# Larger step budgets in attention slots 9 to 17, smaller ones from slot 18 on, and four output-projection items behind one gate

## The chip, the cores and the metric

The kernel runs on one core of one Trainium2 chip. The metric is device time in microseconds (us); lower is better. A profile of one execution gives, for every instruction, its start and its length on one of five engines: PE (TensorE: matrix products, with the weight loads counted apart as PEld), DVE (VectorE), ACT (ScalarE), POOL (GpSimd) and SP (which issues the DMAs). Each engine works through its own instructions in program order; semaphores make one engine wait for another.

## The reference, cut to what matters

One layer of a hybrid encoder is computed for 512 prompt rows and 64 sample rows (576 in all, width 1024). Two kinds of attention stand side by side: four differential heads (two softmax maps each) and four latent heads, whose queries, keys and values are first expanded from normalised latents. Both go into one output projection, and a gated feed-forward network follows.

```
proj = h @ w_in
q_d, k_d = rope(...), rope(...); v_d = ...              # differential heads
c_q, c_kv = rmsnorm(...), rmsnorm(...); k_r = rope(...) # latents, shared rotary key
q_m = c_q @ w_qb;  kv = ckv_all @ w_kvb                 # latent heads, expanded
od = (softmax(s0) - lam * softmax(s1)) @ v              # per differential head
om = softmax(q_nope k_nope^T + q_rope k_rope^T) @ v     # per latent head
x1 = x + concat(od, om) @ w_out
y  = x1 + (silu(conv(g)) * u) @ w_down
```

## The kernel before

Everything is float32; the large products are made of three products of split operands (a high part and a rest), so each product of a 128-row weight tile is a group of three matrix instructions (lines 138 to 140). The attention part is scheduled by hand: under `manual_schedule` the order of the code is the order on each engine.

Attention is a list of 36 blocks (128 queries each, or the sample rows): first 18 differential blocks (`ND` is 18), then 18 latent ones. They pass through a pipeline of slots. In one slot the block before last finishes, the last one is transposed, and a new one begins:

- `combine` (DVE) joins or scales the probabilities of the previous block; `begin` makes the scores of the new one (PE: `S` or `Sm`), their maximum (DVE: `nmax`) and their exponential (ACT: `p`);
- `transpose` turns the previous block's probabilities (PE: `tp`, DVE copy: `pT`);
- `values` multiplies the block before that with its values (PE: `O`, `Os` or `Om`), and after a head's last block a normalisation follows (`osq` on ACT, `orn` on POOL, `ob` and `mixd` on DVE, `ot` on PE).

After each of these three, `Filler.run(us)` puts in products that do not depend on the block, so that PE has something to do while DVE and ACT work on the softmax. They come from the list `fill`, in this order: V0, K1, Q1, V1 (values, keys and queries of differential heads), CQ, CKV, KR (the query latent, the key/value latent and the shared rotary key), QU (rotary part of the latent queries), U0, U1 (expansion of latent heads 0 and 1), VM (values of the latent heads), U2, U3, W0 to W3 (the half of the output projection that the differential heads feed). Each item is cut into steps; a step carries a cost in us by the number of its columns, and `run` takes steps until its budget is used. The budgets stand in `GAPS`: six rows of three, one row for each stretch of slots.

```
gap = GAPS[(slot > ND // 4) + (slot >= ND // 2) + (slot >= 3 * ND // 4) + (slot >= ND) + (slot >= ND + 9)]
filler.need(*needs.get(slot, ()))
```

So the rows hold for slots 0 to 4, 5 to 8, 9 to 12, 13 to 17, 18 to 26 and from 27 on. `needs` says what has to be complete before a slot may begin: before slot 18, the first with latent scores, CQ, CKV, KR, QU and U0; whatever of them is left is issued there in one piece. An item named in `gates` is passed over until the gate is lifted: VM until the last differential block has given its values (slot 19), W0 until slot 20. At the start of W0 `residual()` issues the four DMAs that bring x again.

Some work rides along with the steps: the splitting of weights that later items need (`wqr`, `wqn`, `wkv`, `wo`: high part on ACT, rest on DVE or POOL), and chains called sides, that are moved on by one at every few steps (normalising and splitting the latents: `lsq`, `ncol`, `rc`, `rbc`, `lc`, `lat`; splitting the rotary key and queries: `kr`, `qr`). The products of the fill list share three PSUM buffers under the tag `acc`, and `ncol` and `rbc` of the sides use the same three; a fourth product waits until DVE or ACT has read the oldest.

Of the kernel before, what the change touches and what calls it, by code (L numbers as in the profile page):

```python
# [36 lines left out]

GAPS = ((1.0, 1.0, 1.0), (1.2, 1.2, 1.2), (0.8, 1.2, 1.2), (0.9, 0.9, 0.9), (0.8, 1.1, 1.1), (0.9, 1.0, 0.9))  # L40
NORM_STEPS = (3, 1, 4, 2)
LATE_STEPS, ROPE_STEPS, KEY_STEPS, ROW_STEPS, FIRST_WEIGHTS = 10, 2, 4, 3, 3
SPLIT_EVERY = {"V1": 3, "U1": 2, "KR": 2, "CKV": 3, "QU": 3, "U0": 2}
# [21 lines left out]
def stream_step(ctx: ExitStack, tc: tile.TileContext, i, o):  # L65
# [34 lines left out]
    class Weights:  # L100
        def __init__(self, src, n, name, parts=1, raw=None, own=None):
            self.raw = raw_tile(name + "r") if raw is None else raw
            self.ready = self.begun = False
            if own is None:
                self.place(name)
            else:
                self.hi, self.lo = own
            self.cols = parts if isinstance(parts, list) else [
                slice(n * m // parts, n * (m + 1) // parts) for m in range(parts)]
            self.src = src  # L110
            if parts == 1 and raw is None:
                self.load()
# [824 lines left out]
    class Filler:  # L937
        def __init__(self):
            self.credit = 0.0
            self.count = 0  # L940
            self.name = "start"
            self.done = set()
            self.gates = {"VM", "W0"}
            self.sides = []
            self.gen = None
            self.specs = [w for item in fill for w in item[1]]
            self.loaded, self.todo = [], []
            for _ in range(3):
                self.load()
# [99 lines left out]
    filler = Filler()  # L1049
# [40 lines left out]
    if True:  # L1090
        filler.need("V0")
        tails = []

        def resume():
            for t in list(tails):
                if next(t, "end") == "end":
                    tails.remove(t)

        at = {}
        for n, blk in enumerate(blocks):  # L1100
            at[n, 0] = blk
            at[n + 1, 1] = blk
            at[n + 2, 2] = blk
        needs = {ND // 2: ("K1", "Q1"), ND // 2 + 2: ("V1",), ND: ("CQ", "CKV", "KR", "QU", "U0"),
                 ND + 2: ("U1",), ND + 4: ("U2",), ND + 6: ("U3",)}
        for slot in range(max(k[0] for k in at) + 2):
            a, b, c = (at.get((slot, n)) for n in range(3))
            gap = GAPS[(slot > ND // 4) + (slot >= ND // 2) + (slot >= 3 * ND // 4) + (slot >= ND) + (slot >= ND + 9)]
            filler.need(*needs.get(slot, ()))
            if slot == ND:  # L1110
                filler.finish("key", "rope0")
            if slot == ND + 4:
                filler.finish("rope1")
            if b:
                b.combine()
            resume()
            if a:
                a.begin()
            filler.run(gap[0])
            if b:  # L1120
                b.transpose()
            resume()
            filler.run(gap[1])
            if c is blocks[ND]:
                filler.need("VM")
            if c:
                c.values()
            resume()
            if c and c.finish is not None:
                t = c.finish()  # L1130
                if t is not None:
                    next(t)
                    tails.append(t)
            if c is blocks[ND - 1]:
                filler.gates.discard("VM")
            if slot == ND + 2:
                filler.gates.discard("W0")
            filler.run(gap[2])
        filler.need("W3")
    order.close()  # L1140
# [458 lines left out]
```

## Time and profile before

| | |
|---|---|
| median of 3 runs | 680.38 us (680.08 to 680.64) |
| the profiled execution | 680.18 us |
| its span, first to last instruction | 678.0 us |
| busy PE / PEld / DVE / ACT / POOL | 657.3 / 632.4 / 508.4 / 314.6 / 119.5 us |
| granted PE clock, mean | 0.995 |

The span is what the profile shows from the first to the last instruction; 2.2 us of the execution lie around it. Busy times are sums of instruction lengths with overlaps removed. A matrix instruction is pipelined: its length in a row is longer than the distance to the next start, so PE that is called busy can still be fed more or less densely, but PE that is idle had nothing to do or waited. The slots do not appear in the profile by number; each begins with its score products, so slot 9 begins at 98.73 us, slot 14 at 125.93, slot 17 at 142.99, slot 18 at 166.15 and slot 22 at 190.60.

### The profile page before, as it was taken

To read this page: it belongs to the slowest core of one execution; us is meant where nothing else is said; L and a number is where in the kernel's file an instruction comes from. 1 tells how busy PE (TensorE), PEld (TensorE's weight loads), DVE (VectorE), ACT (ScalarE), POOL (GpSimd) and SP (SyncE) were. 2 spreads that over 40 slices of the span, in tenths; PEclk is the share of its full clock that TensorE was granted. 3 is DMA by queue.
4 is the path that set the end of the run, shared out by engine and by line. 5 is a ranking of instruction groups with operands and counts; after the bars stand their busy time and mean duration, and the time that the engine had idled before them with its cause. 6 is when DMAs were issued, how large, how long until landed. Compare 5 with 4: busy or idle time off the path is not lost.

```text
span 678.0 us, 12372 instructions
## 1 busy us (share of the span) xinstructions
PE 657.3 (97%) x4830; PEld 632.4 (93%) x4830; DVE 508.4 (75%) x1030; ACT 314.6 (46%) x630; POOL 119.5 (18%) x170
## 2 busy tenths in 40 slices
PE   8999999997899999999999999999999999999995
PEld 7998888996799899999999999999999999999994
DVE  5768866588667757899999859884894798697524
ACT  7424345444634345475665236432740552564152
POOL 0130213035200016152130101110110010011042
PEclk9999999999999999999999999999999999999997
DMA  8554413012514113012233303330431133114004
GB/s 286 184 164 151 133 36 113 23 32 89 201 33 155 32 32 125 1 37 89 66 123 125 125 1 124 126 112 13 143 131 38 49 109 125 54 57 143 31 1 141
DMA packets 26858, 63.63 MB, mean 94 GB/s; under 512 B 3248, under 2 KB 8304, under 8 KB 26800
## 3 DMA queue, kind: packets, MB, share of 16 engines
q1 hardware_dynamic: 26800, 62.85, 28.3%
q8 instruction: 38, 0.62, 0.4%
q14 instruction: 20, 0.16, 0.1%
HBM read 55.27 MB, written 5.21 MB: 89 GB/s over the span
## 4 chain that ended last, share of the span: by engine, by line
PE 83%; DVE 10%; ACT 3%; issue 2%; POOL 1%; DMA 1%; SPq 0%; POOLq 0%; DVEq 0%; ACTq 0%
PE yacc L138 9%; PE yacc L139 9%; PE yacc L140 9%; PE ua L1248 6%; PE ua L1246 6%; PE ua L1247 6%; PE ub L1248 3%; PE ub L1247 3%; PE ub L1246 3%; PE uc L1248 2%; PE uc L1247 2%; PE uc L1246 2%; PE uplain L138 1%; PE S L489 1%; PE uplain L139 1%
## 5 line engine op out<-in xcount | busy, mean ns | idle before, releaser
L83 DVE TENSOR_TENSOR x<-x,yacc 128x288 f32<-128x288 f32 (+2 forms) x128 | 56.3, 449 | 52.3 <-PE yacc L140 52.0
L138 PE MATMUL yacc<-act,wd 128*128 128x288 f32 x288 | 85.2, 296 | 0.0
L139 PE MATMUL yacc<-act,wd 128*128 128x288 f32 x288 | 85.1, 295 | 0.0
L140 PE MATMUL yacc<-act,wd 128*128 128x288 f32 x288 | 85.0, 295 | 0.0
L139 PEld LDWEIGHTS yacc<-act,wd 128*128 128x128 f32 x288 | 54.3, 189 | 0.0
L138 PEld LDWEIGHTS yacc<-act,wd 128*128 128x128 f32 x288 | 54.3, 189 | 0.0
L140 PEld LDWEIGHTS yacc<-act,wd 128*128 128x128 f32 x288 | 54.3, 188 | 0.0
L1274 POOL COPY cst<-G 128x2 f32<-128x2 f32 x22 | 23.1, 1052 | 166.9 <-DVE G L83 150.9
L1335 ACT COPY u<-ua 128x288 f32<-128x288 f32 x20 | 8.0, 400 | 66.9 <-PE ua L1248 66.9
L457 ACT ACTIVATE p<-S,nmax 128x128 f32<-128x128 f32 (+4 forms) x36 | 18.6, 516 | 42.1 <-DVE nmax L455 41.7
L86 DVE SCALAR_TENSOR_TENSOR conv<-G,vec,conv 128x578 f32<-128x578 f32 x44 | 35.9, 815 | 2.4 <-ACT conv L1279 2.3
L1261 POOL COPY G<-zero 128x2 f32<-128x2 f32 x22 | 9.6, 438 | 129.0 <-DVE conv L86 120.3
L83 POOL TENSOR_TENSOR n<-n,nsq 128x288 f32<-128x288 f32 x13 | 12.3, 950 | 75.1 <-ACT nsq L865 74.9
L457 ACT ACTIVATE p<-Sm,nmax 128x128 f32<-128x128 f32 (+4 forms) x18 | 9.3, 516 | 29.1 <-DVE nmax L455 29.1
L1279 ACT ACTIVATE conv<-G,vec 128x578 f32<-128x578 f32 x22 | 19.1, 870 | 7.0 <-DVE G L83 6.9
L83 POOL TENSOR_TENSOR st<-pr 128x256 f32<-128x256 f32 (+1 forms) x16 | 13.4, 858 | 49.6 <-issue 16.9
L865 ACT ACTIVATE nsq<-x 128x288 f32<-128x288 f32 (+2 forms) x28 | 12.3, 441 | 17.8 <-DVE x L83 17.7
L89 ACT CAST act<-conv 128x576 fp32r<-128x576 f32 x22 | 14.8, 675 | 11.4 <-DVE conv L83 11.3
L469 DVE COPY pT<-tp 128x128 f32<-128x128 f32 (+3 forms) x36 | 16.6, 462 | 4.3 <-PE tp L466 3.8
L1283 ACT ACTIVATE silu<-conv 128x578 f32<-128x578 f32 x22 | 15.2, 689 | 10.1 <-DVE conv L86 10.1
L455 DVE TENSOR_REDUCE nmax<-S 128x1 f32<-128x128 f32 (+4 forms) x36 | 16.9, 475 | 1.1
L466 PE MATMUL tp<-ident,p 128*128 128x128 f32 x84 | 15.3, 276 | 2.5 <-DVE p L779 1.1
(1595 smaller groups left out, 2552.7 us busy)
## 6 DMA issues: line engine op xcount, KB each, us to landing
qkT<-st SPq DMA_DIRECT2D x32, 72.0 KB, 2.1
x<-in_xT SPq DMA_DIRECT2D x4, 576.0 KB, 6.3
xraw<-in_xT SPq DMA_DIRECT2D x7, 288.0 KB, 5.9
out_kd<-st SPq DMA_DIRECT2D x4, 288.0 KB, 2.4
out_y<-x SPq DMA_DIRECT2D x3, 384.0 KB, 3.1
out_vp<-vd SPq DMA_DIRECT2D x2, 512.0 KB, 4.5
out_y<-x SPq DMA_DIRECT2D x4, 192.0 KB, 2.4
wq0r<-in_w_in SPq DMA_DIRECT2D x2, 256.0 KB, 5.7
```

Source lines behind the costliest of these rows:

```text
L83: (eng or nc.vector).tensor_tensor(out=out, in0=a, in1=b, op=op)
L86: nc.vector.scalar_tensor_tensor(out=out, in0=a, scalar=s, in1=b, op0=op0, op1=op1)
L138: nc.tensor.matmul(out, lhsT=wh, rhs=xh, start=first, stop=False)
L139: nc.tensor.matmul(out, lhsT=wh, rhs=xl, start=False, stop=False)
L140: nc.tensor.matmul(out, lhsT=wl, rhs=xh, start=False, stop=last)
L455: nc.vector.tensor_reduce(out=nmax[:, 0:1], in_=Sv, axis=AX.X, op=ALU.max, negate=True)
L457: nc.scalar.activation(out=p[:, :nk], in_=Sv, func=AF.Exp, bias=nmax[:, 0:1], accum_out=sums)
L1246: nc.tensor.matmul(acc, lhsT=wh, rhs=xh, start=first and n == 0, stop=False, skip_group_check=True)
L1247: nc.tensor.matmul(acc, lhsT=wh, rhs=xl, start=False, stop=False, skip_group_check=True)
L1248: nc.tensor.matmul(acc, lhsT=wl, rhs=xh, start=False, stop=(n == len(ks) - 1), skip_group_check=True)
L1274: nc.gpsimd.tensor_copy(out=cst[:, j, 0:2], in_=G[:, 512:514])
L1279: nc.scalar.activation(out=c[:, :578], in_=G[:, 0:578], func=AF.Identity, scale=cw[0], bias=cb)
```

## The change

The third and fourth rows of `GAPS` grow (slots 9 to 12 from 0.8, 1.2, 1.2 to 1.3, 1.5, 1.4; slots 13 to 17 from 0.9 each to 1.5, 1.5, 1.4), the fifth and sixth shrink (slots 18 to 26 from 0.8, 1.1, 1.1 to 0.8, 1.0, 1.0; from 27 on from 0.9, 1.0, 0.9 to 0.7, 0.9, 0.8). W1 to W3 now stand behind the same gate as W0, so that none of them can come before W0 and before the DMAs of x.

```diff
-GAPS = ((1.0, 1.0, 1.0), (1.2, 1.2, 1.2), (0.8, 1.2, 1.2), (0.9, 0.9, 0.9), (0.8, 1.1, 1.1), (0.9, 1.0, 0.9))
+GAPS = ((1.0, 1.0, 1.0), (1.2, 1.2, 1.2), (1.3, 1.5, 1.4), (1.5, 1.5, 1.4), (0.8, 1.0, 1.0), (0.7, 0.9, 0.8))
...
-            self.gates = {"VM", "W0"}
+            self.gates = {"VM"} | {f"W{fp}" for fp in range(4)}
...
-                filler.gates.discard("W0")
+                filler.gates -= {f"W{fp}" for fp in range(4)}
```

No instruction is added or taken away, and the order among the fill steps stays as it was but for VM: U2 and U3 are finished before its gate opens, where before it stood between them. What moves is the attention blocks among the steps. Before, when slot 18 begins, 4 steps of KR, 9 calls of QU and 5 of U0 are left and are issued in one piece. Now U0 ends in the second third of slot 17, three steps of U1 follow there, and nothing is left at slot 18.

PE, at the end of QU and the beginning of U0 (`qracc` are the rotary query products, `qnacc` the first products of U0). Before, nothing stands between them; here is the end of it and what follows:

```order
L138 MATMUL qracc<-lat,wqrh 128x320
L139 MATMUL qracc<-lat,wqrh 128x320
L140 MATMUL qracc<-lat,wqrl 128x320
L138 MATMUL qnacc<-lat,wqnh 128x256
L139 MATMUL qnacc<-lat,wqnh 128x256
L140 MATMUL qnacc<-lat,wqnl 128x256
```

Now the scores of the last differential block (slot 17, the sample rows of the second pair of heads) stand there:

```order
L138 MATMUL qracc<-lat,wqrh 128x320
L139 MATMUL qracc<-lat,wqrh 128x320
L140 MATMUL qracc<-lat,wqrl 128x320
L532 MATMUL S<-qkT 64x192 x4
L138 MATMUL qnacc<-lat,wqnh 128x256
L139 MATMUL qnacc<-lat,wqnh 128x256
L140 MATMUL qnacc<-lat,wqnl 128x256
```

In the same way the scores, transposes and value products of slots 15 and 16 have come between the products of KR and QU.

DVE, in slot 15 (`lat` is the split of the latents, `pr` the evacuation of KR's or QU's products, `wqnl` the rest of a weight split, `ob` and `mixd` the normalisation of a differential head). One piece of the difference:

```order
 L83 TENSOR_TENSOR pr<-kracc,sinr 64x256
-L83 TENSOR_TENSOR lat<-lc,lat 128x576 x2
+L505 RECIPROCAL c_1823<-sums 128x1
+L86 SCALAR_TENSOR_TENSOR c_1823<-sums,nlam,c_1823 128x1
+L86 SCALAR_TENSOR_TENSOR p<-p,c_1823 128x256
+L86 SCALAR_TENSOR_TENSOR oms<-sums 128x4
+L86 SCALAR_TENSOR_TENSOR oms<-oss,oms 128x4
+L453 MEMSET S 64x64
+L455 TENSOR_REDUCE nmax<-S 128x1
```

A block's combination and maxima now stand inside the work that KR and QU give to DVE.

DVE, further on, at the boundary of slots 15 and 16 (`c` and `p` are the combination of slot 16, `nmax` its maxima):

```order
 L83 TENSOR_TENSOR wqnl<-wqnr,wqnh 128x512 x2
 L86 SCALAR_TENSOR_TENSOR pr<-qracc,cos 128x256
 L86 SCALAR_TENSOR_TENSOR pr<-qracc,msin 128x256
+L505 RECIPROCAL c_1944<-sums 128x1
+L86 SCALAR_TENSOR_TENSOR c_1944<-sums,nlam,c_1944 128x1
+L86 SCALAR_TENSOR_TENSOR p<-p,c_1944 128x384
+L453 MEMSET S 64x64
+L455 TENSOR_REDUCE nmax<-S 128x1
+L453 MEMSET S 64x64
+L455 TENSOR_REDUCE nmax<-S 128x1
 L86 SCALAR_TENSOR_TENSOR lc<-lc,vec,rbc 128x256
 L83 TENSOR_TENSOR q<-pr 128x256
```

The instruction that writes `lc` reads `rbc` and so frees one of the three `acc` buffers; it now comes behind a whole block's combination and maxima.

## Rows read from the trace of the kernel before

**Rows 1.** The page: busy us, share and instructions; PE and clock by slice.

```profile
PE 657.3 (97%) x4830; PEld 632.4 (93%) x4830; DVE 508.4 (75%) x1030; ACT 314.6 (46%) x630; POOL 119.5 (18%) x170
...
PE   8999999997899999999999999999999999999995
...
PEclk9999999999999999999999999999999999999997
```

**Rows 2.** Stretches between slots: busy us (instructions) per engine, clock, DMA, GB/s.

```profile
98.73:142.99 44.26, 44.26 (x326) 38.63 (x325) 27.40 (x88) 20.17 (x67) 8.84 (x9) 1.00 0.17 52
142.99:166.15 23.16, 19.76 (x146) 18.01 (x145) 19.99 (x43) 12.06 (x27) 10.97 (x11) 1.00 0.26 88
166.15:190.60 24.45, 21.52 (x138) 18.17 (x138) 16.98 (x49) 15.46 (x49) 5.79 (x8) 1.00 0.39 140
190.60:224.93 34.33, 34.33 (x264) 33.74 (x263) 25.79 (x69) 12.46 (x30) 0.00 (x0) 1.00 0.30 93
```

**Rows 3.** PE's waits, 142.99 to 190.6 us: total us, times, longest.

```profile
PE qracc L138 <- DVE pr L86: 1.9, 1, 1.9
PE Sm L763 <- ACT knp L737: 1.2, 1, 1.2
PE tp L466 <- DVE p L779: 1.1, 1, 1.1
PE vmacc L747 <- ACT vm L750: 0.6, 1, 0.6
```

**Rows 4.** Timeline of PE at its longest wait: start, us, instruction, idle before.

```profile
153.59 0.38 PE L188 MATMUL rbc<-ident,rc 128*128 128x128 f32 x2
155.84 0.41 PE L138 MATMUL qracc<-lat,wqrh 128*128 128x320 f32 x1 [1.87 <-DVE pr L86]
156.09 0.31 PE L139 MATMUL qracc<-lat,wqrh 128*128 128x320 f32 x1
156.24 0.31 PE L140 MATMUL qracc<-lat,wqrl 128*128 128x320 f32 x1
```

**Rows 5.** DVE by form, 142.99 to 166.15 us: busy us, mean ns, idle before.

```profile
L83 DVE TENSOR_TENSOR lat<-lc,lat 128x576 fp32r<-128x576 f32 x3 | 3.6, 1227 | 0.0
L83 DVE TENSOR_TENSOR wqnl<-wqnr,wqnh 128x512 fp32r<-128x512 f32 x2 | 2.0, 1020 | 0.0
...
L83 DVE TENSOR_TENSOR wqrl<-wqrr,wqrh 128x512 fp32r<-128x512 f32 x2 | 1.4, 676 | 0.0
...
L86 DVE SCALAR_TENSOR_TENSOR pr<-qracc,cos 128x256 f32<-128x256 f32 x2 | 0.8, 424 | 0.0
...
L83 DVE TENSOR_TENSOR pr<-kracc,sinr 64x320 f32<-64x320 f32 x1 | 0.5, 493 | 0.0
...
L86 DVE SCALAR_TENSOR_TENSOR c<-sums,nlam,c 128x1 f32<-128x1 f32 x1 | 0.2, 220 | 0.0
...
L178 DVE TENSOR_SCALAR ms<-ncol 128x4 f32<-128x4 f32 x1 | 0.1, 143 | 0.0
```

**Rows 6.** DVE by form, 98.73 to 190.6 us: the pieces of a differential block.

```profile
L86 DVE SCALAR_TENSOR_TENSOR mixd<-ot,gsub,mixd 128x512 fp32r<-128x512 f32 x3 | 2.2, 750 | 4.4 <-ACT mixd L573 4.4
L455 DVE TENSOR_REDUCE nmax<-S 128x1 f32<-128x384 f32 x4 | 2.2, 557 | 0.1
L83 DVE TENSOR_TENSOR ob<-O,orn 128x512 f32<-128x512 f32 x3 | 2.0, 678 | 0.0
...
L469 DVE COPY pT<-tp 128x256 f32<-128x256 f32 x3 | 1.2, 413 | 0.0
...
L86 DVE SCALAR_TENSOR_TENSOR p<-p,c 128x256 f32<-128x256 f32 x2 | 1.0, 485 | 0.1
```

**Rows 7.** Timeline of POOL beside that wait.

```profile
153.42 2.62 POOL L83 TENSOR_TENSOR kro<-pr 32x320 f32<-32x320 f32 x2
```

**Rows 8.** Timeline of PE: scores, transposes, column sums, two products of QU.

```profile
130.95 0.92 PE L489 MATMUL S<-qkT 64*128 64x384 f32 x4
140.31 0.49 PE L466 MATMUL tp<-ident,p 128*128 128x128 f32 x3
149.21 1.15 PE L166 MATMUL ncol<-ones,lsq 128*128 128x1 f32 x10
...
153.23 0.28 PE L138 MATMUL qracc<-lat,wqrh 128*128 128x256 f32 x1
153.35 0.28 PE L139 MATMUL qracc<-lat,wqrh 128*128 128x256 f32 x1
```

## The prediction

> **What bounds the kernel now.** The page comes first: PE is busy for 97% of the span at full clock in all but one slice [rows 1]. Idle time of PE is therefore the only thing a reordering can win here, since the change neither adds nor removes an instruction. Next come the stretches between slots [rows 2]. PE is idle nowhere from slot 9 to slot 16 (44.26 of 44.26 us busy) nor from slot 22 to 29 (34.33 of 34.33). Between them lie two stretches with idle time: slot 17 with the piece issued before slot 18 (23.16 − 19.76 = 3.40 us) and slots 18 to 21 (24.45 − 21.52 = 2.93 us), 6.33 us together. Each stop also costs the refilling of the pipeline: at the longest, the start after the wait comes 0.25 us before its successor, while the next two starts are 0.15 apart [rows 4], so a stop of 1.87 us costs about 0.1 us more. With some ten stops that makes 7.3 us, the most that can be won.
>
> The waits tell what stands behind it [rows 3]. In the first stretch it is 1.9 us for DVE, which had not yet read a QU product, and 1.2 us for ACT, which had not yet written U0's keys. In slots 18 to 21 it is 1.1 us for a combination on DVE, and the rest are small ones, of which the longest is for ACT in VM. In the first stretch DVE is busy for 19.99 of 23.16 us [rows 2], and in most of it without a gap: this is a piece in which PE and DVE have nearly the same amount of work and each step waits for the one before. In slots 9 to 16 DVE is busy for 27.40 of 44.26 us, so there it has 16.9 us to spare.
>
> **The change part by part.** *The smaller budgets from slot 18 on* take no cover away that is needed: PE stays fully busy in slots 22 to 29 before, the same steps are done by slot 29 in both orders, and slots 18 to 26 still have a budget of 2.8 us each, those from 27 on 2.4. I cost this at nothing; the cover is the W items, and if it were too thin, the wait would be that for `tp`, 1.1 us at its longest in a latent slot [rows 3]. *The gate on W1 to W3* only keeps the order; the DMAs of x are issued a slot earlier in PE's terms, and stand behind the same weight loads on SP, so their cost is nothing too.
>
> *The piece before slot 18 is gone.* Its 18 steps, and three of U1, now lie in slots 14 to 17 among the blocks. What is won is the wait for U0's keys (1.2 us): U0 ends in slot 17, with three steps of U1, value products and the rest of the slot between it and the first latent scores. So is the small wait on the way.
>
> *The work on DVE is the question.* QU, the latents' normalisation and the weight splits are heavy for DVE, and so are differential blocks. I count slot 15 of the new order, the heaviest. DVE: two splits of latents, 2 × 1.23 = 2.45 us; two of `wqn`, 2 × 1.02 = 2.04; one of `wqr`, 0.68; two evacuations of QU, 2 × 0.42 = 0.85; two of KR, 2 × 0.49 = 0.99; small ones, eight of 0.14 to 0.22, 1.3 [rows 5]; the block's own pieces: two maxima of 384 columns, 1.11, the combination 0.49, the copy of the transposes 0.41, `ob` 0.68 and `mixd` 0.75 [rows 6]. That is 11.7 us. Lengths overlap: in the stretch of [rows 5] its 27 groups add up to some 22.4 us where the engine was busy for 19.99 [rows 2], a factor of 0.89. So slot 15 needs 10.4 us on DVE. PE in the same slot, by starts: scores 0.85 (the next instruction starts at 131.80), 24 products of KR of 320 columns at 0.147 = 3.5 [rows 4], ten column sums 1.1, six transposes and a value product about 0.9, 12 products of QU at 0.12 = 1.4 [rows 8], and 0.2 for restarts: 8.0 us. Slots 16 and 17 counted in the same way come to 9.1 and 6.3 on DVE against 7.6 and 6.5 on PE; slot 14 to 6.4 against 7.0. So in slots 15 to 17 DVE has 25.8 us to do where PE has 22.1: it is 3.7 us short, whatever the order inside. PE can run ahead by what the three `acc` buffers hold, about a step or 0.9 us (six products at 0.147). About 2.8 us of stops remain there. The first place should be the second `rbc` of the key/value latent in slot 16, which needs the buffer of the first, and that is read behind a combination (0.9) and two maxima of 512 columns (1.4, an estimate from the 0.56 of 384).
>
> In slots 18 to 21 the same U, VM and W steps stand, with nearly the same total, and ACT still has to do four squares of the head's normalisation, the expansions and splits. I keep 1.2 us of the 2.9: the waits for U0's keys and their rest are gone from this stretch, those for the combination and for VM stay. The new idle time is then 2.8 + 1.2 = 4.0 against 6.33, and with two stops fewer 0.2 more: a gain of 2.5 us. Bounds: if DVE goes by plain lengths without the overlap (25.8 / 0.89 = 29.0 against 22.1, less 0.9, plus 1.2) idle time would be 7.2, a loss of 0.9; if PE's lead covers the whole shortage and the latent slots run clean, the whole 7.3 us are won. I lean a little to the good side, since with blocks and steps mixed each wait has other work behind it, and take 3.0 us.
>
> A price that POOL sets: `wqnl` took 1.02 us where `wqrl` of the same shape took 0.68 [rows 5], with POOL adding two pieces of the rotary key for 2.62 us beside it [rows 7]. The same POOL work is done in the new order, spread over more time, so I keep the means as they are. The Trainium skill, "SBUF — State Buffer", section "SBUF: two separate sides", says that a DVE instruction with two SBUF inputs and a GpSimd instruction that reads SBUF exclude each other for the whole instruction. By that rule each of the two would have waited for a POOL piece of 1.3 us; the trace shows 0.34 us more each, so the rows agree with a contention and not with its size.
>
> **The rivals.** *All of it is won*: DVE works through its queue faster than the means say, because POOL's pieces no longer fall on its weight splits, and PE's lead carries over three slots. For it: 16.9 us of DVE time to spare in slots 9 to 16. Against it: that time comes before the heavy work, and most of DVE's work cannot be done before PE's products. It would give a gain of 5 to 7.3 us, 673 to 675.4.
>
> *Nothing is won*: the stops only move. DVE is short by 3.7 us, less 0.9 of lead; it also waits itself now and then, 3.17 of 23.16 us in the piece before [rows 2], of which a third, 1.1, may come again; slots 18 to 21 keep all their 2.93. Then 6.8 us stand against 6.33, within 1.4 us of before.
>
> *Slower*: DVE takes its work strictly in order, so a block's combination waits behind the weight splits, `tp` on PE waits for it, the steps behind `tp` too, and DVE then waits for their products. If DVE idles as it did in the piece before (19.99 of 23.16 busy, 0.86), slots 15 to 17 take 25.8 / 0.86 = 30.0 us against 22.1, 7.9 of stops; with 2.9 in slots 18 to 21 that is 10.8 against 6.33 and about 4 us slower, 684. It decides from the point at which stops in slots 14 to 17 exceed 4.8 us (3.4 + 1.4). For it: the slots are denser on DVE by 30% than PE's work. Against it: before, DVE idled at the end of the piece, when nothing but U0's chain through ACT was left; now other work stands there.
>
> That the change would not do what it says is excluded by the order: no step is left when slot 18 begins.
>
> **How the numbers follow.** The profiled execution took 680.18 us (678.0 of span and 2.2 around it), 0.2 below the median of 680.38, so a difference in its stretches is carried over to the median: 680.4 − 3.0 = 677.4. Chances: a partial gain of 1.4 to 5 us 0.47, all won 0.19, nothing won 0.20, slower 0.14. The likeliest case's own range is 675.4 to 679.0. For 8 in 10 the range takes in most of the full gain and the case of no gain: 673.0 to 681.0. A difference of 0.2%, 1.4 us, is about what a measurement of this kernel can tell from no change; so faster by more than that 0.66, within it 0.20, slower 0.14.
>
> **What would show it.** Right: no idle PE between the end of U0 and the first latent scores; PE's idle time in slots 14 to 17 between 2 and 4 us, nearly all of it in 15 to 17 and released by DVE; DVE without gaps there; slots 9 to 13 and 22 to 29 without idle PE as before, the feed-forward part of the same length. Wrong: stops in slots 14 to 17 near zero (DVE's count is too high) or above 4.8 us (its order is the bound); new waits for `tp` in slots 21 to 29 (the smaller budgets cost something); waits of ACT for weight DMAs in slots 9 to 13, where the items now follow each other faster.

## The result

The changed kernel takes 689.83 us (median of 4 runs, 688.79 to 690.74) where the kernel before took 680.51 (4 runs, 680.08 to 680.88) beside it: a ratio of 1.0133, with a 95% interval of 1.0115 to 1.0151. It is slower by 9.3 us. The forecast was 677.4, at most 681.0. One execution of the kernel before, in the third group of experiments below, took 1278.58 us; no ratio and no mean contains it.

| | before | after |
|---|---|---|
| the profiled execution | 680.18 us | 690.74 us |
| its span | 678.0 us | 689.0 us |
| busy PE / PEld / DVE | 657.3 / 632.4 / 508.4 us | 663.9 / 638.0 / 508.6 us |
| granted PE clock, mean | 0.995 | 0.986 |

The number of instructions is the same, yet PE is busy for 6.6 us longer. The page of the changed kernel says where to look (compare [rows 1]): the last line is PE's clock by slice, and the tenth of the 40 slices (155 to 172 us) stands at 8, where the kernel before has 9.

```profile
PE 663.9 (96%) x4830; PEld 638.0 (93%) x4830; DVE 508.6 (74%) x1030; ACT 315.7 (46%) x630; POOL 117.2 (17%) x170
...
PE   8999999988699999999999999999999999999995
...
PEclk9999999998999999999999999999999999999998
```

The stretches between slots of the changed kernel (slots 9 to 16, 17, 18 to 21, 22 to 29; answers to [rows 2], though the slots hold other steps now), and three stretches inside them; the columns are length, busy PE, PEld, DVE, ACT and POOL with instruction counts, PE's clock, DMA share, GB/s:

```profile
97.99:165.50 67.51, 64.07 (x438) 56.12 (x437) 45.00 (x117) 28.28 (x80) 16.86 (x18) 0.92 0.20 65
165.50:174.92 9.42, 7.59 (x53) 6.08 (x53) 6.64 (x17) 4.55 (x14) 1.86 (x3) 1.00 0.00 0
174.92:203.40 28.48, 22.42 (x141) 19.63 (x140) 15.67 (x50) 15.54 (x47) 4.70 (x6) 0.94 0.34 120
203.40:235.80 32.40, 32.31 (x247) 31.49 (x245) 23.28 (x64) 12.67 (x30) 0.00 (x0) 1.00 0.31 99
133.09:136.50 3.41, 3.41 (x13) 2.43 (x12) 0.94 (x5) 0.35 (x1) 1.82 (x2) 0.50 0.02 5
156.99:163.81 6.82, 6.51 (x29) 5.63 (x28) 6.78 (x13) 5.59 (x10) 1.68 (x1) 0.50 0.32 112
191.12:194.53 3.41, 3.41 (x15) 3.01 (x14) 2.74 (x9) 1.22 (x6) 0.56 (x1) 0.50 0.08 32
```

Two things are to be read here. PE is idle for 67.51 − 64.07 = 3.44 us up to slot 16, 1.83 in slot 17 and 6.06 in slots 18 to 21, 11.33 in all against 6.33 in [rows 2]: 5.0 more. And PE runs for 3.41 + 6.82 + 3.41 = 13.64 us at a granted clock of 0.50, the level of 1.2 GHz, where in [rows 2] all four stretches stand at 1.00. From slot 30 to the end both kernels take 453 us (689.0 − 235.8, 678.0 − 224.9), and up to slot 9 the changed kernel is 0.7 us ahead, so the whole difference lies here.

PE's waits from 140 to 200 us (line waited for, total us, times, longest), to be held against [rows 3]:

```profile
PE ot L571 <- DVE ob L83: 3.5, 2, 2.3
PE tp L466 <- DVE Sm L453: 2.3, 1, 2.3
PE qracc L138 <- DVE pr L86: 1.9, 1, 1.9
PE tp L466 <- DVE p L779: 1.4, 1, 1.4
PE knacc L138 <- DVE qnl L86: 1.3, 1, 1.3
```

The wait of 1.9 us for a QU product is the one of [rows 3], no shorter; the wait of 1.2 us for U0's keys is gone; four new ones have come, all for DVE (the two for `ob`, the one of 2.3 and that for `qnl`); and the wait for `p` of 1.1 us is one of 1.4. The row of 2.3 us names `Sm` (L453) because that is DVE's next instruction behind the `p` that PE needs. Two of the new waits can be followed on DVE's timeline (start, us, instruction, idle before and its releaser):

```profile
176.68 0.69 DVE L83 TENSOR_TENSOR knl<-knacc,knp 128x512 fp32r<-128x512 f32 x1 [1.42 <-ACT knp L737]
177.29 0.15 DVE L505 RECIPROCAL c<-sums 128x1 f32<-128x1 f32 x1
177.47 0.22 DVE L86 SCALAR_TENSOR_TENSOR c<-sums,nlam,c 128x1 f32<-128x1 f32 x1
177.73 0.42 DVE L86 SCALAR_TENSOR_TENSOR p<-p,c 128x192 f32<-128x192 f32 x1
...
188.63 0.43 DVE L86 SCALAR_TENSOR_TENSOR qnl<-qnacc,qn 128x256 fp32r<-128x256 f32 x1 [2.61 <-POOL qr L83]
188.97 0.28 DVE L469 COPY pT<-tp 128x128 f32<-128x128 f32 x1
189.17 0.68 DVE L83 TENSOR_TENSOR ob<-O,orn 128x512 f32<-128x512 f32 x1
```

The combination that slot 18's transposes wait for (`p`, 177.73) stands behind the split of U1's keys (`knl`), which waits 1.42 us for ACT; the three steps of U1 that came into slot 17 brought it there. And `ob` stands behind a piece of U3, `qnl`, which had to wait 2.61 us for POOL: it takes the buffer that holds the second pair of rotary queries `q`, and POOL was still splitting them (`qr`).

The clock can be seen on PE's timeline of the changed kernel, first around its stop in slot 16, then around 133 us:

```profile
153.30 0.43 PE L188 MATMUL rbc<-ident,rc 128*128 128x128 f32 x2
155.59 0.41 PE L138 MATMUL qracc<-lat,wqrh 128*128 128x320 f32 x1 [1.86 <-DVE pr L86]
155.84 0.31 PE L139 MATMUL qracc<-lat,wqrh 128*128 128x320 f32 x1
...
157.29 0.47 PE L139 MATMUL qracc<-lat,wqrh 128*128 128x320 f32 x1
157.55 0.47 PE L140 MATMUL qracc<-lat,wqrl 128*128 128x320 f32 x1
...
129.66 2.17 PE L166 MATMUL ncol<-ones,lsq 128*128 128x1 f32 x20
131.76 0.41 PE L138 MATMUL lacc<-xh,wi10h 128*128 128x320 f32 x1
...
133.52 0.47 PE L139 MATMUL lacc<-xl,wi10h 128*128 128x320 f32 x1
133.79 0.47 PE L140 MATMUL lacc<-xh,wi10l 128*128 128x320 f32 x1
```

At the full level a product of 320 columns takes 0.31 us and the next starts 0.15 later; from 156.99 on it is 0.47 and 0.27. The first fall follows a stop. The second follows no stop at all: PE is busy without a break from slot 9 to the end of slot 14, and ahead of this fall it had run 20 column sums of one column each, 2.17 us in a row. Nor does every stop bring a fall: behind the longest, the 2.34 us before slot 18's transposes, the clock stays at 1.00.

### The profile page after: what moved, and what is told of

It is laid out like the page before. It is cut to its first block, busy times and chain, and to the rows that moved or that the text cites. A ratio compares the mean times of both kernels' runs of the same rounds, so it can differ in the third digit from the quotient of the medians.

```text
span 689.0 us, 12366 instructions
## 1 busy us (share of the span) xinstructions
PE 663.9 (96%) x4830; PEld 638.0 (93%) x4830; DVE 508.6 (74%) x1030; ACT 315.7 (46%) x630; POOL 117.2 (17%) x170
## 4 chain that ended last, share of the span: by engine, by line
PE 80%; DVE 11%; ACT 3%; issue 2%; POOL 1%; DMA 1%; SPq 0%; POOLq 0%; DVEq 0%; ACTq 0%
PE yacc L138 9%; PE yacc L139 9%; PE yacc L140 9%; PE ua L1248 6%; PE ua L1246 6%; PE ua L1247 6%; PE ub L1248 3%; PE ub L1247 3%; PE ub L1246 3%; PE uc L1248 2%; PE uc L1247 2%; PE uc L1246 2%; PE uplain L138 1%; PE uplain L139 1%; PE uplain L140 1%
## 5 line engine op out<-in xcount | busy, mean ns | idle before, releaser
L1274 POOL COPY cst<-G 128x2 f32<-128x2 f32 x22 | 21.6, 980 | 164.3 <-DVE G L83 148.3
L86 DVE SCALAR_TENSOR_TENSOR conv<-G,vec,conv 128x578 f32<-128x578 f32 x44 | 35.8, 815 | 2.4 <-ACT conv L1279 2.4
L466 PEld LDWEIGHTS tp<-ident,p 128*128 128x128 f32 x84 | 10.6, 145 | 8.4 <-issue 3.4
```

The costliest lines, as they stand in the source:

```text
L86: nc.vector.scalar_tensor_tensor(out=out, in0=a, scalar=s, in1=b, op0=op0, op1=op1)
L466: nc.tensor.transpose(out=pt_ps[:, n * P:n * P + P], in_=a[:, c:c + P], identity=ident)
L1274: nc.gpsimd.tensor_copy(out=cst[:, j, 0:2], in_=G[:, 512:514])
```

## The experiments

Fourteen runs were made, thirteen of variants and one of the kernel before, in four groups, each group with its own executions of the kernel before. For each stands the median and the ratio to the kernel before in the same group with its interval; kernels of different groups are compared by these ratios. Each run has one profile, of one execution. At the end stands one account of all the profiles.

**Which part of the change costs it.** Three kernels hold one part of it each, and a fourth tries a buffer. The expectations speak of theory A (the late slots: U's steps ahead of combinations, and a clock that falls behind the stops), theory B (any larger budget ahead of slot 18 leaves DVE short in slots 13 to 17) and theory C (the buffer of the rotary queries).

`row3`: the third row alone (and the gate).

```diff
-GAPS = (..., (0.8, 1.2, 1.2), (0.9, 0.9, 0.9), (0.8, 1.1, 1.1), (0.9, 1.0, 0.9))
+GAPS = (..., (1.3, 1.5, 1.4), (0.9, 0.9, 0.9), (0.8, 1.1, 1.1), (0.9, 1.0, 0.9))
```

> Only the budgets of slots 9 to 12 are raised; the other rows stay as before (the gate on W1 to W3 stands). 11 calls of the piece before slot 18 are left instead of 18, and QU and U0 are still issued without blocks between them. Theory A (the loss comes from the late slots: expansion steps U in front of the combinations of slots 17 to 19, and QU among the blocks of 15 and 16, with the clock falling after the stops): no loss, 679 to 681.5, at most one stop over 1 us in slots 14 to 21 more than before, and the clock never at half level before the end. Theory B (any raised budget before slot 18 makes DVE short of time in slots 13 to 17): 683 to 686.

687.96 us, 1.0087 (1.0057 to 1.0117): slower than either theory said. Its profile has half-level stretches at 133.8, 154.3 and 185.0 us (3.41 each) and 2.7 us more idle time.

`row4`: the fourth row alone, (1.5, 1.5, 1.4).

> Only the budgets of slots 13 to 17 are raised. Four calls of U0 are left before slot 18; no step of U1 comes into slot 17; QU lies among the blocks of slots 16 and 17. Theory A: the stops in slots 15 to 17 are there as in the changed kernel (some 5 us idle with the piece of U0), those of slots 18 to 20 are near those of before (2.9 us) and the half clock is shorter than the 13.7 us of the changed kernel: 683 to 686. Theory B: all of the loss, 688 to 690.

686.91 us, 1.0085 (1.0051 to 1.0119). Here the stretch of slots 9 to 29 tells most, with two pieces of it:

```profile
97.78:231.93 134.15, 126.44 (x870) 112.75 (x869) 90.69 (x245) 60.94 (x170) 24.45 (x27) 0.95 0.25 82
152.76:159.58 6.82, 5.60 (x27) 4.32 (x27) 5.60 (x13) 0.09 (x1) 3.58 (x4) 0.50 0.55 178
169.82:176.65 6.83, 6.21 (x23) 5.70 (x24) 3.90 (x12) 2.08 (x8) 1.32 (x2) 0.50 0.24 77
```

PE is idle for 134.15 − 126.44 = 7.71 us, only 1.4 more than before, but the stretch is 7.95 us longer (the sum of [rows 2] is 126.20). The rest is 13.65 us at half level. Either row alone brings most of the loss, and the two do not add up: A, which expected no loss from the third row, falls; B named the right rows, but set the price of the third too low (683 to 686) and that of the fourth too high (688 to 690).

`rows56`: only the smaller budgets from slot 18 on (and the gate).

> Only the two last rows are lowered (slots from 18 on), with the gate on W1 to W3. All 18 calls stay in one piece before slot 18. Both theories: within 0.2% of before, 679.5 to 682; if the smaller budgets take cover away in the latent slots, 682 to 685 with new waits for tp in slots 21 to 29.

681.88 us, 1.0009 (0.9986 to 1.0033): no difference that can be told. The smaller budgets cost nothing, as forecast.

`late4`: the changed kernel, with the splits of the second pair of rotary queries begun earlier.

```diff
-LATE_STEPS, ROPE_STEPS, KEY_STEPS, ROW_STEPS, FIRST_WEIGHTS = 10, 2, 4, 3, 3
+LATE_STEPS, ROPE_STEPS, KEY_STEPS, ROW_STEPS, FIRST_WEIGHTS = 4, 2, 4, 3, 3
```

> The changed kernel with one number more changed: the split of the second pair's rotary queries begins 4 steps after QU instead of 10. Theory C: the 2.29 us stop at 189.9 us (value of ob) stands behind a product evacuation of head 3 on DVE, which waits 2.6 us for its buffer, and that buffer still holds the rotary queries of the second pair, which POOL is splitting; with the split begun earlier that stop is gone and the half clock at 191 us with it: 685.5 to 688. Rival: the evacuation waits for ACT or for PE's product, and the buffer has nothing to do with it: 689 to 691, with the stop still there.

688.30 us, 1.0089 (1.0053 to 1.0124). The wait for `ob` of 2.3 us is gone (1.2 is the longest left) and so is the half-level stretch behind it; 1.5 us less than the changed kernel's median, but in another group, and the intervals of the two ratios overlap. C holds for its one stop.

**Two of the stops, and PE's clock.** The second group asks whether the stops can be taken away, and whether they take the clock down.

`u1late4`: `late4`, and U1 to U3 held back until slot 18.

```diff
-            self.gates = {"VM"} | {f"W{fp}" for fp in range(4)}
+            self.gates = {"VM", "U1", "U2", "U3"} | {f"W{fp}" for fp in range(4)}
...
+            if slot == ND:
+                filler.gates -= {"U1", "U2", "U3"}
```

> The changed kernel with U1 to U3 held back until slot 18 begins, so that the last differential block's combination on DVE no longer stands behind U1's key split, and with LATE_STEPS 4 in place of 10, so that the splits of the rotary queries are done before head 3 needs their buffer. It puts theory A of the earlier runs (three steps of U1 ahead of that combination cost 2.34 us) beside its rival that another wait takes the place. Theory A: the stop for tp of 2.34 us and that for ob of 2.29 us are gone and that of 1.43 is shorter, idle time of PE in slots 14 to 21 is 6 to 7 us against 11.3, one or two of three half-level stretches go with it: 683 to 685.5. Rival: the steps that no longer stand in slot 17 leave slot 17 without cover, PE waits for U0's keys as the kernel before did, idle time stays above 9 us: 686.5 to 688.5, no better than with LATE_STEPS alone.

688.52 us, 1.0118 (1.0104 to 1.0132). PE's waits from 140 to 200 us:

```profile
PE qracc L138 <- DVE pr L86: 2.1, 2, 1.9
PE ot L571 <- DVE ob L83: 1.9, 2, 1.2
PE tp L466 <- DVE oms L86: 1.5, 1, 1.5
PE knacc L138 <- DVE qnl L86: 1.3, 1, 1.3
PE tp L466 <- DVE p L86: 1.0, 1, 1.0
PE Sm L763 <- ACT knp L737: 0.6, 1, 0.6
```

The stop of 2.3 us for slot 18's transposes is gone, so its cause was named rightly. But a combination in slot 17 (1.0), U0's keys (0.6) and another late one (1.5) have taken its place. The rival holds: no better than `late4`.

`again`: the kernel before, one more profile.

> The kernel before, unchanged, one more look. Theory K: in an execution whose mean clock is below 0.994 a half-level stretch lies behind one of its two stops in slot 17 (1.87 and 1.2 us), with PE's idle time as in the first profile, 6.3 us, and the span is longer than 677.5 by 0.45 to 0.5 us per us of it. Theory I: such stretches lie elsewhere, or the longer span goes with more idle time.

The stretch of slots 15 and 16 of this profile, then of the first profile of the same program:

```profile
129.64:143.25 13.61, 13.61 (x88) 11.95 (x87) 7.55 (x22) 5.67 (x14) 3.48 (x4) 0.87 0.02 7
134.43:137.84 3.41, 3.41 (x15) 3.41 (x15) 0.37 (x1) 0.30 (x1) 0.00 (x0) 0.50 0.02 5
168.56:171.97 3.41, 3.41 (x14) 3.03 (x13) 1.85 (x6) 2.01 (x7) 0.00 (x0) 0.50 0.38 145
```

```profile
130.95:142.99 12.04, 12.04 (x88) 10.38 (x87) 7.35 (x22) 5.48 (x14) 3.48 (x4) 1.00 0.03 7
```

The same 88 matrix instructions without idle time take 12.04 us at full clock and 13.61 with 3.41 us of it at half level: 0.46 us are lost for each us at half level. So the kernel before loses clock too, in some of its executions: one stretch right behind its column sums (134.43), one behind its stops in slot 17 (168.56). Theory K named the second place and not the first. Its other number fails: 6.82 us at half level should have made the span at least 3.1 us longer than 677.5, and it is 1.7 (679.2). The stretch of slots 9 to 29 is 2.97 us longer than in the first profile, but what stands ahead of it and behind it is 1.8 shorter.

`padafter`: unread products in the stops of the changed kernel.

```diff
+    def pad(kind, out=None):
+        n = PADS.get((kind, pad_at["slot"]), PADS.get((kind, None), 0))
+        if n and out is None:
+            out = psum("T", "pad")
+        for _ in range(n):
+            nc.tensor.matmul(out[:, :P], lhsT=ones, rhs=ones, start=True, stop=True)
```

> The changed kernel with 35 products that nothing reads (128x128, the form of the spin at the program's start) put in PE's order right before the places where it stops: 4 before the transposes of ob in slot 15, 6 behind the first rbc of the key/value latent, 4 before the first key products of U0, 8 and 5 before tp in slots 18 and 19, 8 before the transposes of ob in slot 19. The rest is as in the changed kernel. At 0.25 us each (an estimate: half of the 0.49 that one takes at the half clock level at the start) they fill 8.6 of some 10.4 us of stops and add no time where a stop is longer. Theory K (PE's stops also take the granted clock down, and this costs as much as the stops): the half-level stretches at 157 (6.83 us) and 191 (3.41 us) disappear, that at 133 stays, since nothing is put there; 10.2 us at about 0.45 us lost per us are won, at most 0.5 us is lost where products outlast a stop: 685 to 686.5. Theory I (the stops alone cost the time, the clock falls have another cause or cost nothing): the clock stays as it was and the time is that of the changed kernel or a little more, 689.5 to 691.

695.29 us, 1.0222 (1.0207 to 1.0238): missed by both. PE's timeline at three of the six places:

```profile
151.91 1.50 PE L166 MATMUL pad<-ones 128*128 128x128 f32 x12
153.66 0.41 PE L138 MATMUL qracc<-lat,wqrh 128*128 128x320 f32 x1 [0.24 <-DVE pr L86]
...
169.68 2.08 PE L166 MATMUL pad<-ones 128*128 128x128 f32 x8 [2.93 <-DVE pT L480]
177.53 1.97 PE L166 MATMUL tp<-ones 128*128 128x128 f32 x16
```

At the first the products filled the stop, and the half-level stretch behind it was gone. At the second they waited 2.93 us for the PSUM buffer that they share with the transposes, a new stop, and around it the clock was at half level (167.18 to 174.01). The time does not decide between the theories.

`padbefore`: the same in the two stops of the kernel before (6 behind the first `rbc`, 4 before the first latent scores).

> The kernel before with ten such products: 6 behind the first rbc of the key/value latent (the stop of 1.87 us) and 4 before the first latent scores (the stop of 1.2 us). Theory K: where the kernel before ran beside others, its executions spread from 679.2 us at a mean clock of 0.995 to 684.3 at 0.988, because the clock falls in some of them behind these stops. With them filled the mean clock is 0.993 or more in most executions and the median 679 to 680.5, below that of the kernel before in the same rounds by 1 to 2 us, and the spread is smaller. Theory I: no gain, the same time or up to 1 us more.

679.64 us, 0.9988 (0.9975 to 1.0001). Of 11 executions six stand at a mean clock of 0.995 with spans of 676.5 to 677.5, and five at 0.991 to 0.993 with 679.1 or 679.2. The profiled one is of the second kind: its only half-level stretch ahead of the end of the program is the one behind the column sums, at 135.29; behind the filled stops the clock stays up. This is the fastest kernel of the study, 1.1 us ahead of the kernel before; its interval just reaches no difference.

**Is the stop one of DVE's order, or of its amount of work?** The third group moves a weight split, and cuts the column sums in two. Theory D is the order, theory S the column sums.

`wqnafter` (the changed kernel) and `wqnbefore` (the kernel before): the splits of `wqn` spread over QU's steps.

```diff
...
-        ("QU", [(i["w_qb"][:, 1024:], 1024, "wqr"), (i["w_qb"][:, 0:1024], 1024, "wqn")], q_up),
-        ("U0", [(i["w_kvb"], 1024, "wkv")], ...),
+        ("QU", [(i["w_qb"][:, 1024:], 1024, "wqr")], q_up),
+        ("U0", [(i["w_qb"][:, 0:1024], 1024, "wqn"), (i["w_kvb"], 1024, "wkv")], ...),
...
```

> The changed kernel with one weight (wqn) moved in the list of items from QU, which does not use it, to U0, which does: the splits of wqn are then spread over QU's steps, where before all of them were issued ahead of QU's first step. On DVE the two pieces wqnl (2.10 us together in the profile of the changed kernel, 153.10 to 155.20) no longer stand ahead of the two evacuations of QU for which PE's stop of 1.86 us at 155.59 waits. Theory D (the stop is one of DVE's order, and the half-level stretch of 6.83 us from 156.99 follows it): the stop is below 0.4 us, no half-level stretch follows there, the splits later cost at most 0.5: a gain of 1.4 to 1.9 from idle time and about 3 from the clock, 684.5 to 686. Rival (DVE's amount of work is the bound, and the stop only moves): the same 1.4 us and more come back as a stop later in slots 16 and 17, and the clock falls there: 688.5 to 690.

688.61 us, 1.0111 (1.0088 to 1.0134). The stop of 1.86 us for QU is gone, with the half-level stretch behind it; but these have come or grown (the changed kernel has none for `wkvh`, 0.3 for `rbc` and 0.2 for `p` of L86), and a half-level stretch of 6.83 us with them, from 167 us on:

```profile
PE knacc L138 <- ACT wkvh L124: 1.8, 1, 1.8
...
PE rbc L188 <- DVE lc L86: 1.2, 1, 1.2
PE tp L466 <- DVE p L86: 1.0, 1, 1.0
```

> The kernel before with wqn moved in the same way. Theory D: the stop of 1.87 us in slot 17 goes to below 0.4, that for U0's keys (1.25 and 0.40) stays, so 1.4 us are won, and where the clock fell behind this stop another 1.4: median 678.5 to 679.5 where the kernel before has 680.5 to 681.5 in the same rounds. Rival: the work on DVE is the bound of slot 17, the stop comes back ahead of U0's keys: the same as before within 0.5 us.

682.99 us, 1.0031 (1.0014 to 1.0048): slower. The stop of 1.87 us is gone, two of 0.9 have come, and PE's idle time in slots 9 to 29 is 6.16 us against 6.33. What rose is the time at half level: the mean clock of 12 executions is 0.990, that of the kernel before beside them 0.993. In both kernels the stop only moves, as the rivals say; but the rival for `wqnbefore` expected the time to stay within 0.5 us, and 2.2 us were lost.

`halfwqnafter` and `halfbefore`: the column sums in two groups with a step of products between them.

```diff
-            pc = sum_cols(sqs, T, "acc")
+            pc = sum_cols(sqs, T, "acc", None, range(2))
+            yield 1
+            sum_cols(sqs, T, "acc", pc, range(2, 5))
             yield NORM_STEPS[1]
...
```

> The same, and the 20 column sums of the latents' normalisation (2.17 us in a row on PE) in two groups of 8 and 12, with one step of products between. Theory S (column sums in a row take the clock down): in the changed kernel the half-level stretch of 3.41 us at 133.09 follows 20 column sums, with no stop of PE ahead of it. With two groups none follows, and 1.4 us more are won than by wqn alone. Rival: that stretch has another cause; it stays, and the time is that with wqn alone, within 0.5 us.

> The kernel before with the column sums in two groups of 8 and 12, nothing else. Theory S: in two profiles of kernels with the order of before the clock falls right behind the 20 column sums (at 134.43 and 135.29), in the first it does not; it should fall there in no execution, so the median is 0.5 to 1.2 us below that of the kernel before in the same rounds, with the executions at a mean clock of 0.991 or less gone or fewer. Rival: no difference, within 0.3 us.

688.68 us, 1.0116 (1.0087 to 1.0144), and 683.16 us, 1.0034 (1.0018 to 1.0050). In both profiles no half-level stretch stands behind the sums, as theory S has it. That makes S likely and no more: of the twelve profiles in which the 20 sums stand in a row, nine have such a stretch at them and three (`before`, `rows56`, `padafter`) have none. And nothing is won. `halfbefore` is slower by 2.4 us, which neither theory expected, and six of its 12 executions have a mean clock of 0.991 or less (three of the 22 of the kernel before). The normalisation comes a step later, QU's first products wait for the latents' split (1.76 and 1.40 us in the two profiles), and the clock falls there. The profile of `halfwqnafter` is of its slowest execution (692.01 us).

**Once more, with products only where they bring no wait.**

`padafter2` (the changed kernel; 6, 8 and 5 products) and `padrow4` (`row4`; 4, 3 and 4).

> The changed kernel with the unread products only at three places where, in the run before with them, they stood inside a stop and brought no wait of their own: 6 behind the first rbc of the key/value latent, 8 before tp in slot 18, 5 before tp in slot 19 (1.50, 1.97 and 1.27 us there, in place of stops of 1.86, 2.34 and 1.43). The two places where the products had to wait for the PSUM buffer of the transposes themselves (2.93 and 1.69 us) are left out. Theory K: the half-level stretch of 6.83 us that followed the first stop disappears, that at 191 becomes rarer; that behind the column sums (3.41 at 133) stays: mean clock 0.990 or more instead of 0.9865, time 685.5 to 687.5 against 689.8, though PE does 4.7 us more work. Theory I: the clock falls have another cause; the mean clock is as before and the time 689.5 to 691.

690.50 us, 1.0129 (1.0103 to 1.0154). The mean clock of the 6 executions is 0.9895 against 0.9865, so some of the half-level time went, but for 4.7 us of products PE's idle time fell by only 2.4 (11.42 to 9.07): stops came back behind them. Theory K was near on the clock and missed the time, which lies where theory I put it.

> The kernel with the larger budgets in slots 13 to 17 alone, and unread products before its stops of 1.22 us (4, behind the first rbc), 0.73 (3, before U0's key products) and 1.24 (4, before the first latent scores). That kernel has no more idle time of PE than the kernel before (6.4 against 6.3 us in the profiles) and is 0.85% slower. Theory K: the stretch of 6.83 us at half level from 169.82 disappears, that from 152.76 stays, since it follows stops of 0.16, 0.72 and 0.41 us at QU's start, where nothing is put: 2.5 to 3 us faster than without the products, 683.5 to 685. Theory I: 686.5 to 688.

685.57 us, 1.0058 (1.0041 to 1.0075), where `row4` had 1.0085 (1.0051 to 1.0119); the two intervals overlap. Theory K expected 683.5 to 685, theory I 686.5 to 688. The profile is of the fastest of the 12 executions (683.79), and in it the clock is full from slot 9 to slot 29:

```profile
97.61:228.77 131.16, 124.26 (x891) 111.01 (x891) 90.69 (x245) 60.63 (x169) 24.46 (x27) 1.00 0.25 84
```

Against the profile of `row4` that is 2.2 us less busy PE, though the 11 products (22 instructions) came on top, and 3.0 us less time. Not all of it can be put down to the products: the half-level stretch of `row4` at 152.76 is missing too, and ahead of that place stand no products but the same short stops (0.17, 0.72 and 0.41 us). Theory K had expected it to stay. The executions tell more than this one profile: `row4` has mean clocks of 0.983 to 0.990 (5 executions, 0.9864 in the mean), `padrow4` of 0.990 to 0.994 (12, 0.9918), while the kernel before has 0.9920 and 0.9922 beside them. So products in the stops keep the clock up for a part of the time; most executions still lose some of it.

**One account of the profiles.** The stretch from the start of slot 9 to that of slot 30, from the same view: its length, PE's idle time in it (length less busy PE), the time of it at half level, and what comes out if the 126.20 us of the kernel before are taken and the additional idle time, 0.46 us for each us at half level and the unread products are added.

| kernel | length | idle | half level | worked out |
|---|---|---|---|---|
| before | 126.20 | 6.33 | 0 | |
| after | 137.83 | 11.42 | 13.64 | 137.6 |
| row3 | 134.18 | 9.00 | 10.2 | 133.6 |
| row4 | 134.15 | 7.71 | 13.65 | 133.9 |
| rows56 | 128.25 | 7.01 | 3.4 | 128.4 |
| late4 | 135.50 | 10.33 | 10.2 | 134.9 |
| u1late4 | 135.46 | 9.65 | 10.2 | 134.2 |
| again | 129.17 | 6.15 | 6.8 | 129.2 |
| wqnafter | 136.58 | 12.04 | 10.2 | 136.6 |
| wqnbefore | 129.88 | 6.16 | 6.8 | 129.2 |
| halfwqnafter | 138.26 | 9.95 | 17.1 | 137.7 |
| halfbefore | 128.57 | 6.65 | 3.4 | 128.1 |
| padbefore (2.6 of products) | 127.80 | 4.08 | 3.4 | 128.1 |
| padafter2 (4.7 of products) | 138.53 | 9.07 | 10.2 | 138.4 |
| padrow4 (3.0 of products) | 131.16 | 6.90 | 0 | 129.7 |

`padafter` is left out, since a part of its products ran at half level. Two terms give every length to within 1.5 us, and the changed kernel's to within 0.3. Length less idle time is busy PE, so what this bears out is the second term: busy PE grows by the price of the clock and by the products put in. What is left over has no term here. Each stop also costs an estimated 0.1 us for the start behind it (0.25 us to the next one in place of 0.15, [rows 4]), and since a product of 320 columns has a length of 0.31 us and a distance of 0.15, a stop below 0.16 does not show as idle time.

**Which stop the falls go with.** Six profiles share the changed kernel's order ahead of the QU stop in slot 16, but for unread products and the `wqn` splits. With the stop (1.86, 1.87 and 1.86 us in `after`, `late4`, `u1late4`) the clock is at half level for 6.82, 6.83 and 3.41 us from within 1.4 us behind it; where it is filled or gone (`padafter`, `padafter2`, `wqnafter`) there is no such stretch. So in this order the stop takes the clock along. It is not so with each stop, nor in each order: the QU stop of 1.87 or 1.88 us in the order of before has no stretch within 5 us behind it in any of three profiles (`before`, `again`, `rows56`); the stop of 2.29 us for `ob` has a stretch at it in `after`, `padafter2`, `row3` and `halfwqnafter` and none in `wqnafter`, and the one for slot 18's transposes none in `after` (2.34) or `late4` (2.21).

## Why the prediction was wrong

**What bounds the kernel: this step failed.** It said that idle time of PE is the only thing that a reordering can win, since PE is at full clock. So the clock was no term of the sum, on either side. In the profiled pair it is the larger one: the stretch of slots 9 to 29 is 11.6 us longer, of which 5.1 are additional idle time and 13.64 × 0.46 = 6.3 the clock. Over the executions it is the smaller one. The four of the changed kernel have spans of 688.0 us at a mean clock of 0.9865; the 15 of the kernel before in the first group of experiments have 679.2 and 0.992, since their clock is not full in all of them either. A mean clock lower by 0.0055 is 2 × 0.0055 × 688 = 7.6 us more at half level, 3.5 us of the 8.8; the other 5.3 are near the additional idle time of the profile. The Trainium skill, page "TensorE: Matmul & The Clock Gate", section "What's actually happening", says that the throttled clock is the default and that activity releases it. The trace agrees in the two levels, 0.50 and 1.00. The falls of the changed kernel came behind stops of 1.86 and 2.29 us, and the one at 133 us behind none.

**Slots 15 to 17: right kind, wrong size.** The count gave 2.8 us of stops, to be seen between 2 and 4; there are 5.27 (3.44 up to slot 16, 1.83 in slot 17), and the forecast had set 4.8 as the point from which the slow rival decides. The three slots of the changed kernel, in the columns used above:

```profile
142.49:152.24 9.75, 8.47 (x60) 7.34 (x59) 8.13 (x21) 4.32 (x10) 3.71 (x5) 1.00 0.04 14
152.24:165.48 13.24, 11.07 (x54) 8.99 (x53) 13.03 (x25) 5.97 (x11) 5.30 (x6) 0.74 0.33 114
165.48:174.92 9.44, 7.62 (x53) 6.10 (x53) 6.66 (x17) 4.55 (x14) 1.86 (x3) 1.00 0.00 0
```

DVE's work was counted at 10.4, 9.1 and 6.3 us and took 8.13, 13.03 and 6.66: the sum is near (25.8 against 27.8), but the heavy slot is 16 and not 15, for the `wqn` splits come there and the two splits of latents in slot 15 took 0.76 us each and not 1.23. PE's count of 22.1 is exceeded by more, 27.2, of which about 3.1 are the clock (6.82 × 0.46). All the stops are released by DVE, as said. The first is earlier than said: `ot` in slot 15 (1.24 us), then the product behind the first `rbc` in slot 16 (1.86), and only then the second `rbc` (0.31). DVE does not go without gaps: it waits 1.30 us for ACT at 148.41 in the changed kernel's profile. In `wqnafter` and `u1late4` a stop taken away comes back at another place, so no single place in DVE's order that was tried is the cause.

**Slots 18 to 21: this step failed too.** It kept 1.2 of 2.9 us, because the wait for U0's keys was gone. 6.06 us were measured. It saw U1's steps in slot 17 as cover and not that U1's key split would stand on DVE ahead of slot 18's combination (2.34), the same with U2 in slot 19 (1.43), nor that U3, now ahead of VM, needs the rotary queries' buffer (2.29).

**The slow rival** had the mechanism: a combination behind other work on DVE, `tp` behind it, the steps behind `tp`. In slots 18 and 19 that work is a split of keys that waits for ACT, and not a weight split. It was right in DVE's busy share (0.86, measured 27.8 of 32.4 us), but that its 10.8 us of idle time meet the 11.33 measured is luck: it had 7.9 in slots 15 to 17 (5.27 measured) and 2.9 in slots 18 to 21 (6.06). Its 684 lacked the clock.

**Right were** the end of the wait for U0's keys, the smaller budgets (`rows56`), full PE in slots 9 to 14 and 22 to 29, and the unchanged feed-forward part.

**POOL.** The prediction read [rows 5, 7] as 0.34 us more for each of the two `wqnl` splits. That is a mean: in the trace of the kernel before the first took its plain 0.7 us and the second 1.36, and the second ended 0.56 behind POOL's first piece. In the changed kernel two other pieces of DVE stand beside POOL:

```profile
160.88 1.75 DVE L83 TENSOR_TENSOR q<-pr 128x320 f32<-128x320 f32 x1
163.94 1.44 DVE L83 TENSOR_TENSOR q<-pr 128x256 f32<-128x256 f32 x1
```

```profile
160.60 1.68 POOL L83 TENSOR_TENSOR kr<-kro,kr 64x704 fp32r<-64x704 f32 x1 [5.95 <-ACT kr L679]
163.82 1.28 POOL L83 TENSOR_TENSOR qr<-q,qr 64x512 fp32r<-64x512 f32 x1 [1.53 <-ACT qr L693]
```

Another piece of 320 columns takes 0.48 us at 168.41, with POOL idle. Here each DVE instruction ends 0.3 us behind POOL's, so it stood still for nearly the whole of it. The Trainium skill, "SBUF — State Buffer", section "SBUF: two separate sides", calls the port pair that the two engines share an exclusive lock. These rows agree with that, in size too, where the prediction had read a smaller contention. It did not decide: beside and behind the two pieces PE is not idle until 167.8 us, and DVE's busy time over the stretch of slots 9 to 29 is 90.57 us against 90.15, since the latents' splits no longer meet POOL.

**Open** stays why the clock falls at the same place in some executions and not in others. Behind the same column sums it fell in three of the five profiles with the order of before around them (`again`, `padbefore`, `wqnbefore`; not in `before` and `rows56`), and in five of six with that of the changed kernel (not in `padafter`). Open is also why a stop of QU of the same length brings a fall in the order of the changed kernel and none in the order of before.

## What to carry to other kernels

Where PE is busy for 97% and its clock full, the second is a thing that can be lost: here a stop of 1.86 us was followed by 6.82 us at half level, an estimated 3.1 us more (6.82 × 0.46), and 20 one-column sums by 3.41, an estimated 1.6. A block of independent products left together need not be waste: in the kernel before it kept DVE's work for the attention blocks apart from DVE's work for the steps. Count a new step among the blocks by what it puts on DVE ahead of the next combination, and by the buffer that it takes, and not only by its columns on PE. Where time changes and idle time does not, compare the mean clock of the executions before looking for a wait.

## What the runs showed that was not expected

Executions of the same program differ in their clock. Of 15 executions of the kernel before in the first group, spans go from 677.1 us at a mean clock of 0.995 to 682.2 at 0.988; the first three runs of this kernel (680.08 to 680.64) were near the short end. An unread product of 128 columns costs 0.25 us in a stop (1.50 us for the six of `padafter`'s first place, which are 12 instructions) and can pay for itself there, but only where the PSUM bank that it writes is free.
